# Attention by minimum of negated sums, in-order re-layouts, first products on half blocks behind a run on zeros, and a layer norm by square root without GpSimd, in a hybrid encoder layer

## Chip, cores and metric

One core of one Trainium2 chip. The metric is device time of one execution in microseconds (us), as a median over runs.

## What is computed

x is 2048 tokens by 1024 channels, float32. One input projection (1024 to 4608) feeds two mixers; their outputs, 1024 wide together, go through an output projection, and a layer norm closes:

```python
h = x @ w_in + b_in
q_a, k_a, v_a, g_a, q_h, z_fwd, z_bwd, i_h, g_h = split(h)
# group A, 8 heads of 64: neighbourhood attention on a 32 x 64 grid, window 8 x 16
s = q_a . k_a * 64 ** -0.5 + bias           # bias -inf outside the window
p = softmax(s);  o_a = (p . v_a) * silu(g_a)
# group B, 4 heads of 128: gated linear recurrence, one scan per direction
o_h = rms_norm(scan(q_h, k_f, i_h, f) + flip(scan(flip(...)))) * gain * silu(g_h)
y = concat(o_a, o_h) @ w_out + b_out
r = 2 ** 0.25 * x + y
out = (r - mean(r)) * rsqrt(var(r) + 1e-5) * ln_gain + ln_bias
```

## The kernel before

Products that need float32 accuracy are made of three: each operand is split into a high part, rounded to a shorter format (a cast on ScalarE, ACT), and the remainder (a subtraction on VectorE, DVE), and high x high, low x high and high x low are added up in PSUM. `split` (lines 154 and 155) does this for each piece that a DMA on SyncE's queue (SP) has brought.

Tokens come in four blocks of 512 (`TB`). A list of jobs, each 128 output channels for one block of tokens, makes up the input projection: 8 slices of the contraction (`KT`) times 3 products, 24 matmuls of 128 x 512. Jobs of values and gates (`vg`, `v2`) use 128 x 256 matmuls with tokens as rows. Around the jobs, eight units for each half of the tokens (4 recurrence heads, then 4 attention head pairs) do their own work. `projections()` is a generator: the units run, and between their steps `advance` takes so many matmuls of the jobs as filler. So the order on TensorE (PE) is written out by the program, and every matmul and transpose is tied to the one before by `in_order`. What the other engines do is ordered by a scheduler from data dependences and priorities, and each engine works its queue strictly in that order.

At the start, `first_loads` (lines 170 to 187) brings the weights of job 0 (`q` of the first recurrence head) in four pieces of 128 KB and the eight slices of the first token block, 256 KB each, in turns. Job 0 needs all of it. The x pieces land in the pool `raw`, which has 5 buffers, so the later ones wait until earlier ones have been split. Job 1 is `zf` (the forward gate) on the same tokens, with weights loaded by `load_w`; jobs 2 and 3 are `q` and `zf` on the second block.

When a job of attention's q or k is done, ACT copies it out of PSUM with the bias added and with its tokens re-ordered, so that 8 (or 4) rows of the grid at one column lie side by side (`evac_plain`, lines 220 and 222). It reads PSUM in order and writes SBUF with a stride:

```python
nc.scalar.activation(t.rearrange("p (c r) -> p r c", r=8), nat(ps), AF.Identity, bias=...)
```

In attention (`scores`, lines 711 to 726), for each step of 128 queries and two heads, DVE adds the bias to the scores in PSUM and takes the maximum per row (line 721), negates it (722), ACT takes the exponential with that as bias and the sum (723), and DVE divides (724, 725); PE transposes (`turn`), ACT copies (739), and PE multiplies with the values (`weigh`). The result is added to a bias and multiplied into the gate, in place, in the gate's own order (line 753): there the gate is read and written with a stride, and PSUM in order.

At the end comes the output projection, 4 token blocks of 4 tiles of 128 tokens, each with 24 matmuls per half of the channels, and the layer norm of `normalise`: statistics (`bn_stats`, `bn_aggr`), `rsqrt` by a shift and three Newton steps on DVE (lines 249 to 254, eleven small instructions), then subtract the mean and multiply by the gain (line 1003), and multiply by rstd and add the bias (1009), 512 columns at a time, and a store from SP's queue. For the last tile alone, ACT subtracts the mean (line 1000) and GpSimd (POOL) multiplies by the gain (line 1001).

Of the kernel before, what the change touches and what calls it, by code (L numbers as in the profile page):

```python
# [75 lines left out]
def _build():  # L76
# [18 lines left out]
    with tile.TileContext(nc) as tc, ExitStack() as top:  # L95
# [73 lines left out]

        def first_loads():  # L170

            w = wp.tile([P, 2, KT, P], F32R, tag="w", name="wt")
            wraw = [rawp.tile([P, KT // 2, P], F32, tag="raw", name="wraw") for _ in range(2)]
            tiles = []
            for kt in range(KT):
                if kt % 2 == 0:
                    i, o = kt // 4, kt % 4
                    part = wraw[i][:, o:o + 2]
                    nc.sync.dma_start(out=part, in_=w_in[16, :, kt:kt + 2])
                    nc.vector.tensor_copy(out=w[:, 0, kt:kt + 2], in_=part)  # L180
                    nc.vector.tensor_tensor(out=w[:, 1, kt:kt + 2], in0=part, in1=w[:, 0, kt:kt + 2].bitcast(F32), op=ALU.subtract)
                raw = rawp.tile([P, TB], F32, tag="raw", name="xraw")
                nc.sync.dma_start(out=raw, in_=xT_in[kt, :, 0:TB])
                t = xwp.tile([P, 2, TB], F32R, tag="xw", name="xt")
                split(t, raw)
                tiles.append(t)
            return w, tiles
# [101 lines left out]
        def projections():  # L289
# [20 lines left out]
            ws[0, "q"], xts[0] = first_loads()  # L310
            first_consts()
            for m, job in enumerate(jobs):
                n, what, c, tb, key = job
# [314 lines left out]
        def att_unit(half, u, h, ahead):  # L628
# [70 lines left out]
            def scores(j, g):  # L699
# [15 lines left out]
                for hd in range(2):  # L715
                    s = ss[hd]
                    sb = wk("ub", [P, 512])
                    mx = wk("mx", [P, 1], F32)
# [24 lines left out]
            def weigh(j, g):  # L743

                po = ps_tile("ms", "pov")
                for b in range(2):
# [239 lines left out]

        def normalise(rs):
# [5 lines left out]
            for i, (r, r0, stats) in enumerate(rs):  # L993
                nc.vector.bn_aggr(out=mv[:, i], in_=stats)
                if last:
                    nm = wk("nm", [P, 1])
                    nc.vector.tensor_scalar(out=nm, in0=mv[:, i, 0:1], scalar1=-1.0, scalar2=None, op0=ALU.mult)
                for cs in halves:
                    if last:
                        nc.scalar.activation(r[:, cs], r[:, cs], AF.Identity, bias=nm)  # L1000
                        nc.gpsimd.tensor_tensor(out=r[:, cs], in0=r[:, cs], in1=vec01[:, 1, cs], op=ALU.mult)
                    else:
                        nc.vector.scalar_tensor_tensor(out=r[:, cs], in0=r[:, cs], scalar=mv[:, i, 0:1], in1=vec01[:, 1, cs], op0=ALU.subtract, op1=ALU.mult)
            va = wk("va", [P, 2])
            nc.vector.tensor_scalar(out=va[:, 0:n], in0=mv[:, 0:n, 1], scalar1=LN_EPS, scalar2=None, op0=ALU.add)
            rstd = newton_rsqrt(va[:, 0:n], n, "ln")
            for i, (r, r0, stats) in enumerate(rs):
                for cs in halves:
                    nc.vector.scalar_tensor_tensor(out=r[:, cs], in0=r[:, cs], scalar=rstd[:, i:i + 1], in1=vec2[:, cs], op0=ALU.mult, op1=ALU.add)
                    nc.sync.dma_start(out=out[r0:r0 + P, cs], in_=r[:, cs])  # L1010
# [69 lines left out]
```

## Time and profile before

| what | value |
|---|---|
| time, median of 3 runs (range) | 1334.14 us (1333.4 to 1337.19) |
| the profiled execution's own time | 1335.69 us |
| span in the profile | 1333.9 us |
| PE busy | 1305.1 us, 98% |
| DVE busy | 894.6 us, 67% |
| ACT busy | 662.8 us, 50% |
| POOL busy | 67.4 us, 5% |
| chain that ended last | PE 89%, DVE 5%, ACT 2%, DMA 2%, issue 1% |

Busy time of PE includes the modelled length of pipelined matmuls, so 98% says that PE nearly always had work, not that it worked at its peak. The chain that ended last is followed back from the last instruction, at each step to what released it; what is not PE in it is where PE waited, and the ends of the program. The views used below are this chain, the timeline (instructions in order of time, with the idle time before them in brackets and what ended it), the list of PE's waits, the groups by line and shape, and stretches (busy time of each engine between two times).

### The profile page before, as it was taken

To read this page: it belongs to the slowest core of one execution; us is meant where nothing else is said; L and a number is where in the kernel's file an instruction comes from. 1 tells how busy PE (TensorE), PEld (TensorE's weight loads), DVE (VectorE), ACT (ScalarE), POOL (GpSimd) and SP (SyncE) were. 2 spreads that over 40 slices of the span, in tenths; PEclk is the share of its full clock that TensorE was granted. 3 is DMA by queue.
4 is the path that set the end of the run, shared out by engine and by line. 5 is a ranking of instruction groups with operands and counts; after the bars stand their busy time and mean duration, and the time that the engine had idled before them with its cause. 6 is when DMAs were issued, how large, how long until landed. Compare 5 with 4: busy or idle time off the path is not lost.

```text
span 1333.9 us, 25319 instructions
## 1 busy us (share of the span) xinstructions
PE 1305.1 (98%) x9864; PEld 1143.5 (86%) x9864; DVE 894.6 (67%) x2310; ACT 662.8 (50%) x1372; POOL 67.4 (5%) x126
## 2 busy tenths in 40 slices
PE   8999999999999999999999999999999999999996
PEld 6989898999888988989889898988889887788885
DVE  4385666575453364736868768688777778899757
ACT  4264444454464464534555646477776778631000
POOL 0000000011100100000000000000001000000000
PEclk9999999999999999999999999999999999999998
DMA  6121212123434365120323113365454667564201
GB/s 222 56 67 57 70 64 86 56 79 103 128 93 125 85 175 183 44 67 19 102 80 98 64 46 116 101 188 166 141 161 147 180 202 238 192 225 172 108 32 64
DMA packets 92312, 153.46 MB, mean 115 GB/s; under 512 B 9952, under 2 KB 42720, under 8 KB 92192
## 3 DMA queue, kind: packets, MB, share of 16 engines
q1 hardware_dynamic: 84256, 126.94, 30.1%
q0 software_dynamic: 7936, 24.91, 5.5%
q8 instruction: 77, 1.26, 0.4%
q14 instruction: 43, 0.35, 0.1%
HBM read 118.52 MB, written 33.29 MB: 114 GB/s over the span
## 4 chain that ended last, share of the span: by engine, by line
PE 89%; DVE 5%; ACT 2%; DMA 2%; issue 1%; SPq 0%; DVEq 0%; ACTq 0%
PE pj L139 36%; PE pv L139 20%; PE yp L139 13%; PE plev L139 4%; PE pov L139 4%; PE ptr L142 3%; PE S L139 3%; PE po L139 2%; PE pk L142 1%; PE pub L139 1%; PE pu L139 1%; PE pb L139 1%; DVE op L560 1%; DMA xraw<-in_xT_dram 1%; DVE ub L721 0%
## 5 line engine op out<-in xcount | busy, mean ns | idle before, releaser
L139 PE MATMUL pj<-xt,wt 128*128 128x512 f32 x2304 | 587.4, 400 | 7.3 <-ACT xt L154 5.7
L139 PEld LDWEIGHTS pj<-xt,wt 128*128 128x128 f32 x2304 | 419.1, 189 | 90.3 <-ACT xt L154 6.4
L139 PE MATMUL pv<-wv,xt 128*128 128x256 f32 x2304 | 301.4, 286 | 0.0
L139 PEld LDWEIGHTS pv<-wv,xt 128*128 128x128 f32 x2304 | 284.5, 191 | 3.0 <-issue 0.7
L139 PE MATMUL yp<-wo,chi 128*128 128x512 f32 (+1 forms) x528 | 161.3, 386 | 0.0
L471 ACT COPY km<-ST 128x512 f32<-128x512 f32 x96 | 64.3, 670 | 124.1 <-PE plev L139 78.9
L723 ACT ACTIVATE ub<-ub,nm 128x384 f32<-128x384 f32 (+2 forms) x128 | 78.8, 617 | 75.4 <-DVE nm L722 75.1
L139 PEld LDWEIGHTS yp<-wo,chi 128*128 128x128 f32 x528 | 98.1, 188 | 20.4 <-issue 0.7
L155 DVE TENSOR_TENSOR wt<-wraw,wt 128x512 fp32r<-128x512 f32 x82 | 53.9, 686 | 37.7 <-ACT wt L154 37.3
L482 DVE TENSOR_TENSOR ST<-ST,PX 128x512 f32<-128x512 f32 x96 | 66.0, 688 | 16.2 <-ACT qm L473 15.6
L739 ACT COPY op<-ptr 96x384 f32<-96x384 f32 (+3 forms) x128 | 62.0, 526 | 14.0 <-PE ptr L142 13.7
L483 DVE TENSOR_TENSOR ST<-ST,PX 128x512 f32<-128x512 f32 x96 | 65.6, 683 | 0.0
L473 ACT COPY qm<-ST 128x512 f32<-128x512 f32 x96 | 64.0, 667 | 0.0
L142 PE MATMUL ptr<-ident,ub 128*128 128x128 f32 (+1 forms) x448 | 59.6, 273 | 2.9 <-DVE ub L725 2.1
L155 DVE TENSOR_TENSOR wv<-vraw,wv 128x512 fp32r<-128x512 f32 x48 | 31.3, 688 | 46.1 <-ACT wv L154 45.9
L142 PEld LDWEIGHTS ptr<-ident,ub 128*128 128x128 f32 (+1 forms) x448 | 51.3, 133 | 11.1 <-DVE ub L725 2.9
L457 DVE COPY_PREDICATED AH<-masks,plev 128x256 f32<-128x256 uint8 x96 | 42.8, 446 | 26.6 <-PE plev L139 24.3
L230 ACT ACTIVATE ht<-pj,bs_sb 128x512 f32<-128x512 f32 x48 | 33.0, 687 | 52.1 <-PE pj L139 52.0
L154 ACT CAST wt<-wraw 128x512 fp32r<-128x512 f32 x82 | 47.7, 621 | 15.3 <-PE pv L139 8.6
L725 DVE TENSOR_SCALAR ub<-ub,rs 128x384 f32<-128x384 f32 (+2 forms) x128 | 52.5, 423 | 2.9
L139 PE MATMUL plev<-qm,km 128*64 128x64 f32 x1536 | 51.0, 223 | 0.0
L139 PEld LDWEIGHTS plev<-qm,km 128*64 128x64 f32 x1536 | 47.5, 138 | 3.7 <-issue 2.5
(212 smaller groups left out, 1791.0 us busy)
## 6 DMA issues: line engine op xcount, KB each, us to landing
wraw<-in_w_in_dram SPq DMA_DIRECT2D x100, 256.0 KB, 2.8
vraw<-in_w_v_dram SPq DMA_DIRECT2D x48, 256.0 KB, 2.8
xraw<-in_xT_dram SPq DMA_DIRECT2D x32, 256.0 KB, 3.9
craw<-cat SPq DMA_DIRECT2D x32, 256.0 KB, 3.7
PP<-in_rpb_dram SPq DMA_DIRECT2D x16, 384.0 KB, 3.7
PX<-in_rpb_dram SPq DMA_DIRECT2D x16, 384.0 KB, 3.5
vt<-hv POOLq DMA_DIRECT2D x32, 128.0 KB, 2.6
PP<-in_rpb_dram SPq DMA_DIRECT2D x8, 512.0 KB, 3.5
```

What stands on the lines that cost most here:

```text
L139: in_order(nc.tensor.matmul(out, lhsT=lhsT, rhs=rhs, start=start, stop=stop, **kw))
L142: in_order(nc.tensor.transpose(out=out, in_=in_, identity=ident))
L154: nc.scalar.copy(out=hi, in_=raw)
L155: last_split[0] = nc.vector.tensor_tensor(out=lo, in0=raw, in1=hi.bitcast(F32), op=ALU.subtract)
L457: nc.vector.copy_predicated(AH, masks[:, l].unsqueeze(1).to_broadcast([P, 4, HC]), pl)
L471: nc.scalar.copy(out=km.rearrange("p (n h b) -> p n h b", h=2, b=B), in_=mix(ST, 0, 3, B, 0, TB))
L473: nc.scalar.copy(out=qm.rearrange("p (n h b) -> p n h b", h=2, b=B), in_=mix(ST, 1, 2, B, 0, TB))
L482: nc.vector.tensor_tensor(out=S1, in0=S1, in1=pr[:, :, :, 0].unsqueeze(3).to_broadcast([P, 2, m, B]), op=ALU.mult)
L483: nc.vector.tensor_tensor(out=S2, in0=S2, in1=pr[:, :, :, 1].unsqueeze(3).to_broadcast([P, 2, m, B]), op=ALU.mult)
L723: nc.scalar.activation(sb[:, 0:nk], sb[:, 0:nk], AF.Exp, bias=nm, accum_out=sums[:, hd:hd + 1])
L725: nc.vector.tensor_scalar(out=sb[:, 0:nk], in0=sb[:, 0:nk], scalar1=rs[:, hd:hd + 1], scalar2=None, op0=ALU.mult)
L739: nc.scalar.copy(out=PT[0:n, 0:nch].rearrange("p a b -> p (a b)"), in_=pt[0:n, 0:nch * P])
```

## The change

It does five things.

- **Start.** `warm` sets a tile to zero on DVE and multiplies it with itself on PE, seven times 128 x 256 in plain float32, before any load has landed. The result is not used.
- **First products on half blocks.** `first_loads` brings the first token block in two halves of 256 tokens: weights of `q` and the first half in turns (the first two slices alone, the others two in one DMA), then the weights of `zf`, then the second half. The x pieces land in the pool `h` (17 buffers) instead of `raw`. The weights' high parts are now cast by ACT, not DVE. Jobs 0 and 1 become 96 matmuls of 128 x 256 in the order `q` first half, `zf` first half, `q` second half, `zf` second half. The second token block is asked for right behind (`prepare(jobs[2])`).
- **Re-layouts in order.** The evacuations of q and k, and the product with the gate, now write SBUF in order (q and k) or in runs of 32 (gate), and read PSUM with a stride.
- **Minimum of negated sums.** Line 721 makes the negated sum and takes the minimum, which is the negated maximum; the exponential has scale -1. The negation (722) goes.
- **Layer norm.** The eleven small instructions become a square root on ACT, a reciprocal and one Newton step (three instructions) on DVE. In the last tile DVE does what ACT and POOL did, in the order: centre the first half, centre and store the second half last, in two pieces of 256 columns, the first of them stored from ACT's queue.

```diff
+        def warm():
+
+            z = wk("AH", [P, 4, HC], F32).rearrange("p a b -> p (a b)")
+            nc.vector.memset(z, 0.0)
+            ps = ps_tile("ms", "warm")
+            for _ in range(7):
+                mm(ps[:, 0:256], z[:, 0:P], z, True, True)
...
         def first_loads():
...
+            def half(o, kt, n):
+                cs = slice(o * 256, o * 256 + 256)
+                raw = h_tile("xraw").rearrange("p (k t) -> p k t", k=2)
+                nc.sync.dma_start(out=raw[:, 0:n], in_=xT_in[kt:kt + n, :, cs].rearrange("k p t -> p k t"))
+                for k in range(n):
+                    split(tiles[kt + k][:, :, cs], raw[:, k])
+
+            for kt in range(0, KT, 2):
+                part = wraw[kt // 4][:, kt % 4:kt % 4 + 2]
+                nc.sync.dma_start(out=part, in_=w_in[16, :, kt:kt + 2])
+                split(wa[:, :, kt:kt + 2], part)
+                if kt == 0:
+                    half(0, 0, 1)
+                    half(0, 1, 1)
+                else:
+                    half(0, kt, 2)
+            wb = load_w(20)
+            for kt in range(0, KT, 2):
+                half(1, kt, 2)
+            return wa, wb, tiles
...
-                nc.scalar.activation(t.rearrange("p (c r) -> p r c", r=8), nat(ps), AF.Identity, bias=b_sb[:, c:c + 1])
+                nc.scalar.activation(t.rearrange("p (c r) -> p c r", r=8), ps.rearrange("p (r c) -> p c r", c=COLS), AF.Identity, bias=b_sb[:, c:c + 1])
...
-                    t.rearrange("p (a c r) -> p a r c", a=2, r=4),
-                    ps.rearrange("p (a r c) -> p a r c", a=2, r=4),
+                    t.rearrange("p (a c r) -> p a c r", a=2, r=4),
+                    ps.rearrange("p (a r c) -> p a c r", a=2, r=4),
...
+            warm()
+            ws[0, "q"], ws[0, "zf"], xts[0] = first_loads()
             first_consts()
+            prepare(jobs[2])
...
-                        nc.vector.tensor_tensor_reduce(out=sb[:, 0:nk], in0=s[:, 0:nk], in1=bt[:, hd, 0:nk], scale=1.0, scalar=-3e38, op0=ALU.add, op1=ALU.max, accum_out=mx)
-                        nc.vector.tensor_scalar(out=nm, in0=mx, scalar1=-1.0, scalar2=None, op0=ALU.mult)
-                        nc.scalar.activation(sb[:, 0:nk], sb[:, 0:nk], AF.Exp, bias=nm, accum_out=sums[:, hd:hd + 1])
+                        nc.vector.tensor_tensor_reduce(out=sb[:, 0:nk], in0=s[:, 0:nk], in1=bt[:, hd, 0:nk], scale=-1.0, scalar=3e38, op0=ALU.add, op1=ALU.min, accum_out=nm)
+                        nc.scalar.activation(sb[:, 0:nk], sb[:, 0:nk], AF.Exp, bias=nm, scale=-1.0, accum_out=sums[:, hd:hd + 1])
...
-                gate = nat(h["g", g])[:, :, 16 * j:16 * j + 32].rearrange("p r c -> p c r")
+                gate = nat(h["g", g])[:, :, 16 * j:16 * j + 32]
...
-                    out=gate, in0=po[:, 0:2 * P].rearrange("p (c r) -> p c r", r=8), scalar=b_sb[:, 8 + u:9 + u],
+                    out=gate, in0=po[:, 0:2 * P].rearrange("p (c r) -> p r c", r=8), scalar=b_sb[:, 8 + u:9 + u],
...
+            root = wk("va", [P, 2])[:, 0:n]
+            nc.scalar.activation(root, mv[:, 0:n, 1], AF.Sqrt, bias=eps)
...
+            early = [(i, cs) for i in range(n) for cs in halves]
+            late = []
+            if last:
+                early, late = early[:-1], [early[-1]]
+            for i, cs in early:
+                centre(i, cs)
...
+            nc.vector.reciprocal(out=rstd, in_=root)
+            nc.vector.tensor_tensor(out=a, in0=rstd, in1=rstd, op=ALU.mult)
+            nc.vector.scalar_tensor_tensor(out=a, in0=a, scalar=-0.5, in1=va, op0=ALU.mult, op1=ALU.mult)
+            nc.vector.scalar_tensor_tensor(out=rstd, in0=a, scalar=1.5, in1=rstd, op0=ALU.add, op1=ALU.mult)
+            for i, cs in early:
+                store(i, cs, nc.sync)
+            for i, cs in late:
+                centre(i, cs)
+                for k, queue in enumerate((nc.scalar, nc.sync)):
+                    store(i, slice(cs.start + 256 * k, cs.start + 256 * k + 256), queue)
```

Three places show how the order moves. On PE, the start of the program, as a difference (`pj` and `pv` are the banks of jobs, `xt` and `wt` split x and weights, `AH` the zeros):

```order
 L95 UNCONDITIONAL_BRANCH
-L139 MATMUL pj<-xt,wt 128x512 x144
+L139 MATMUL warm<-AH 128x256 x7
+L139 MATMUL pj<-xt,wt 128x256 x96
+L139 MATMUL pj<-xt,wt 128x512 x96
 L139 MATMUL pv<-wv,xt 128x256 x192
```

Seven products on zeros stand in front, and 48 of the first 144 matmuls are cut in two; but for bank numbers nothing else of PE's order differs.

On DVE, a step of attention in the first half, before (`S` scores, `PX` the bias, `ub` the result, `mx` and `nm` the maximum and its negation, `rs` the reciprocal of the sum):

```order
L721 ISA ub,mx<-S,PX 128x384
L721 ISA mx 128x1
L721 ISA ub,mx<-S,PX 128x384
L721 ISA mx 128x1
L722 TENSOR_SCALAR nm<-mx 128x1 x2
L724 RECIPROCAL rs<-sums 128x1
L725 TENSOR_SCALAR ub<-ub,rs 128x384
```

and the same step in the change:

```order
L754 ISA ub,nm<-S,PX 128x384
L754 ISA nm 128x1
L754 ISA ub,nm<-S,PX 128x384
L754 ISA nm 128x1
L756 RECIPROCAL rs<-sums 128x1
L757 TENSOR_SCALAR ub<-ub,rs 128x384
```

The two negations are gone; the rest stands as it stood, though elsewhere splits and other DVE work move by a few places around such steps.

On DVE, the last tile's layer norm in the change, from the aggregated statistics (`mv`) to the end:

```order
L1029 BN_AGGR mv<-stats 128x2
L1034 TENSOR_SCALAR nmr<-mv 128x1
L1038 SCALAR_TENSOR_TENSOR xpair<-xpair,mv,ST 128x512
L1053 RECIPROCAL lny<-va 128x1
L1038 SCALAR_TENSOR_TENSOR xpair<-xpair,mv,ST 128x512
L1054 TENSOR_TENSOR lna<-lny 128x1
L1055 SCALAR_TENSOR_TENSOR lna<-lna,nmr 128x1
L1056 SCALAR_TENSOR_TENSOR lny<-lna,lny 128x1
L1042 SCALAR_TENSOR_TENSOR xpair<-xpair,lny,PP 128x512
L1042 SCALAR_TENSOR_TENSOR xpair<-xpair,lny,PP 128x256 x2
```

Ten instructions after the statistics' own, where before stood thirteen small ones and two of 512 columns, with ACT and POOL beside them; the scheduler has put the second half's centring between the reciprocal and the Newton step.

## Rows read from the trace of the kernel before

**Rows 1.** Page, busy time: engine, us, share of the span, instructions.
```profile
PE 1305.1 (98%) x9864; PEld 1143.5 (86%) x9864; DVE 894.6 (67%) x2310; ACT 662.8 (50%) x1372; POOL 67.4 (5%) x126
```

**Rows 2.** Chain that ended last, first 66 us: start us, us, what.
```profile
7.88 3.88 DMA xraw<-in_xT_dram
12.46 30.64 PE pj L139 x132
43.10 23.03 PE pv L139 x192
```

**Rows 3.** Timeline, first 60 us: start us, us, engine, line, operation, tiles [idle before].
```profile
0.73 1.28 ACT L154 ACT_TABLE_LOAD   x1 [0.73 <-PEq L77]
...
3.20 0.43 DVE L181 TENSOR_TENSOR wt<-wraw,wt 128x256 fp32r<-128x256 f32 x1
...
5.50 1.22 PE L139 MATMUL pj<-xt,wt 128*128 128x512 f32 x2 [5.50 <-ACT xt L154]
...
26.82 0.69 ACT L218 ACTIVATE hp<-pj,b_sb 128x512 f32<-128x512 f32 x1 [1.63 <-PE pj L139]
...
32.26 0.69 ACT L230 ACTIVATE ht<-pj,bs_sb 128x512 f32<-128x512 f32 x1 [3.72 <-PE pj L139]
```

**Rows 4.** Timeline, PE alone, 9 to 12 us.
```profile
8.63 3.62 PE L139 MATMUL pj<-xt,wt 128*128 128x512 f32 x8
```

**Rows 5.** Stretch 4 to 6 us: engines' busy us (x), PEclk, DMA share, GB/s.
```profile
4.00:6.00 2.00, 0.50 (x1) 0.50 (x2) 0.00 (x0) 0.79 (x2) 0.00 (x0) 1.00 0.96 335
```

**Rows 6.** PE's waits, whole span: who <- for whom: us in total, times, longest us.
```profile
PE pk L142 <- DVE ST L483: 2.5, 2, 2.2
PE ptr L142 <- DVE ub L725: 2.1, 2, 1.7
PE S L139 <- ACT hu L236: 1.9, 1, 1.9
PE S L139 <- DVE ST L682: 1.9, 2, 1.1
```

**Rows 7.** Groups by line and shape: xcount, busy us, mean ns, idle before.
```profile
L681 ACT CAST ST<-hp 64x256 fp32r<-64x256 f32 x56 | 20.6, 402 | 6.6 <-PE S L139 6.1
L155 DVE TENSOR_TENSOR xt<-xraw,xt 128x512 fp32r<-128x512 f32 x32 | 21.5, 690 | 12.2 <-ACT xt L154 11.9
L220 ACT ACTIVATE hp<-pj,b_sb 128x512 f32<-128x512 f32 x16 | 19.9, 1244 | 17.9 <-PE pj L139 17.7
L222 ACT ACTIVATE hp<-pj,b_sb 128x512 f32<-128x512 f32 x16 | 19.1, 1193 | 14.4 <-PE pj L139 14.4
L722 DVE TENSOR_SCALAR nm<-mx 128x1 f32<-128x1 f32 x128 | 17.4, 149 | 0.3
L753 DVE SCALAR_TENSOR_TENSOR hu<-pov,b_sb,hu 128x256 f32<-128x256 f32 x24 | 16.2, 676 | 21.0 <-PE pov L139 20.8
L363 DVE TENSOR_TENSOR hv<-pv,bvg 128x256 f32<-128x256 f32 x32 | 13.4, 419 | 40.2 <-PE pv L139 40.2
L218 ACT ACTIVATE hp<-pj,b_sb 128x512 f32<-128x512 f32 x16 | 11.0, 688 | 27.4 <-PE pj L139 27.4
```

**Rows 8.** Stretch 835.2 to 838.5 us, columns as in rows 5.
```profile
835.20:838.50 3.30, 3.23 (x12) 2.97 (x13) 3.22 (x8) 2.48 (x6) 0.00 (x0) 0.50 0.36 99
```

**Rows 9.** Chain that ended last, from 1322 us on.
```profile
1322.74 0.43 DVE xpair L1038
...
1323.66 0.28 DVE mv L994
...
1327.87 0.17 DVE lna L252
```

**Rows 10.** Timeline from 1324 us on, PE left out.
```profile
1324.14 1.33 ACT L1000 ACTIVATE xpair<-xpair,nm 128x512 f32<-128x512 f32 x2 [87.69 <-DVE nm L997]
...
1324.95 2.48 POOL L1001 TENSOR_TENSOR xpair<-xpair,ST 128x512 f32<-128x512 f32 x2 [155.80 <-DVE lna L253]
...
1328.53 1.41 DVE L1009 SCALAR_TENSOR_TENSOR xpair<-xpair,lny,PP 128x512 f32<-128x512 f32 x2
```

More of the change, by code (lines that the diff above doesn't have):

```diff
@@ L168, in load_x @@
             return tiles
+        def warm():
[4 more added lines that the diff above has]
+                mm(ps[:, 0:256], z[:, 0:P], z, True, True)
         def first_loads():
-            w = wp.tile([P, 2, KT, P], F32R, tag="w", name="wt")
+            wa = wp.tile([P, 2, KT, P], F32R, tag="w", name="wt")
             wraw = [rawp.tile([P, KT // 2, P], F32, tag="raw", name="wraw") for _ in range(2)]
[L174 to L187, printed above, removed]
+            tiles = [xwp.tile([P, 2, TB], F32R, tag="xw", name="xt") for _ in range(KT)]
+            def half(o, kt, n):
[17 more added lines that the diff above has]
+            return wa, wb, tiles
         def load_w(c):
@@ L308, in prepare @@
                     ws[key] = load_w(c)
-            ws[0, "q"], xts[0] = first_loads()
+            warm()
+            ws[0, "q"], ws[0, "zf"], xts[0] = first_loads()
             first_consts()
+            prepare(jobs[2])
+            banks = [ps_tile("pj", "pj"), ps_tile("pj", "pj")]
+            for o in range(2):
+                cs = slice(o * 256, o * 256 + 256)
+                for ps, what in zip(banks, ("q", "zf")):
+                    w = ws[0, what]
+                    for kt in range(KT):
+                        for i, (a, b) in enumerate(((0, 0), (1, 0), (0, 1))):
+                            mm(ps[:, cs], w[:, a, kt], xts[0][kt][:, b, cs], kt == 0 and i == 0, kt == KT - 1 and i == 2)
+                            if (kt * 3 + i) % 2 and not (o == 1 and kt == KT - 1 and i == 2):
+                                yield 1
+                    if o == 1:
+                        gots[0][what, 0] = evac_plain(ps, 16) if what == "q" else evac_tanh(ps, 20)
+                        yield 1
             for m, job in enumerate(jobs):
+                if m < 2:
+                    continue
                 n, what, c, tb, key = job
@@ L717, in scores @@
                     sb = wk("ub", [P, 512])
-                    mx = wk("mx", [P, 1], F32)
                     nm = wk("nm", [P, 1], F32)
                     with tc.high_priority(offset=PRIO):
-                        nc.vector.tensor_tensor_reduce(out=sb[:, 0:nk], in0=s[:, 0:nk], in1=bt[:, hd, 0:nk], scale=1.0, scalar=-3e38, op0=ALU.add, op1=ALU.max, accum_out=mx)
-                        nc.vector.tensor_scalar(out=nm, in0=mx, scalar1=-1.0, scalar2=None, op0=ALU.mult)
-                        nc.scalar.activation(sb[:, 0:nk], sb[:, 0:nk], AF.Exp, bias=nm, accum_out=sums[:, hd:hd + 1])
+                        nc.vector.tensor_tensor_reduce(out=sb[:, 0:nk], in0=s[:, 0:nk], in1=bt[:, hd, 0:nk], scale=-1.0, scalar=3e38, op0=ALU.add, op1=ALU.min, accum_out=nm)
+                        nc.scalar.activation(sb[:, 0:nk], sb[:, 0:nk], AF.Exp, bias=nm, scale=-1.0, accum_out=sums[:, hd:hd + 1])
                         nc.vector.reciprocal(out=rs[:, hd:hd + 1], in_=sums[:, hd:hd + 1])
@@ L985, in _build @@
         nc.sync.dma_start(out=vec2, in_=vec_in[2])
+        eps = cp.tile([P, 1], F32, name="eps")
+        nc.vector.memset(eps, LN_EPS)
         def normalise(rs):
@@ L994, in normalise @@
                 nc.vector.bn_aggr(out=mv[:, i], in_=stats)
[L995 to L1010, printed above, removed]
+            root = wk("va", [P, 2])[:, 0:n]
@@ new lines, in normalise, with centre, store @@
+            nc.scalar.activation(root, mv[:, 0:n, 1], AF.Sqrt, bias=eps)
+            va = wk("nmr", [P, 2])[:, 0:n]
+            nc.vector.tensor_scalar(out=va, in0=mv[:, 0:n, 1], scalar1=LN_EPS, scalar2=None, op0=ALU.add)
+            def centre(i, cs):
+                r = rs[i][0]
+                nc.vector.scalar_tensor_tensor(out=r[:, cs], in0=r[:, cs], scalar=mv[:, i, 0:1], in1=vec01[:, 1, cs], op0=ALU.subtract, op1=ALU.mult)
+            def store(i, cs, queue):
+                r, r0, _ = rs[i]
+                nc.vector.scalar_tensor_tensor(out=r[:, cs], in0=r[:, cs], scalar=rstd[:, i:i + 1], in1=vec2[:, cs], op0=ALU.mult, op1=ALU.add)
+                queue.dma_start(out=out[r0:r0 + P, cs], in_=r[:, cs])
@@ new lines, in normalise @@
+            early = [(i, cs) for i in range(n) for cs in halves]
[4 more added lines that the diff above has]
+                centre(i, cs)
+            rstd = wk("lny", [P, 2])[:, 0:n]
+            a = wk("lna", [P, 2])[:, 0:n]
+            nc.vector.reciprocal(out=rstd, in_=root)
+            nc.vector.tensor_tensor(out=a, in0=rstd, in1=rstd, op=ALU.mult)
+            nc.vector.scalar_tensor_tensor(out=a, in0=a, scalar=-0.5, in1=va, op0=ALU.mult, op1=ALU.mult)
```

## Prediction
> **What bounds the kernel now.** I read the page first: PE has work for 98% of the span [rows 1], so an edit pays only where PE waits or where the program has not begun or has ended on PE. Next the chain that ended last: from 12.46 us it is PE with hardly a break [rows 2], and ahead of that it is DMA, the last wait being for a slice of x that took 3.88 us to land. Third the list of PE's waits: after the start, its four largest entries come to 8.4 us in 7 waits, over a run of 1,300 us [rows 6]. Fourth the end: the first DVE step after PE's last matmul is at 1322.74, and from there it is DVE, with ACT and POOL beside it, until 1329.94 [rows 9, 10]; then the last store lands. So there are three places: a head of some 12 us, some 10 us of waits inside, and a tail of 11 us. PE's order in between is the same before and after.
>
> **The head.** How much PE lost there is read from the first full-speed jobs. The third job's result is taken out at 26.82, the next at 32.26 [rows 3]: 5.44 us for 24 matmuls, 227 ns each. So the third job began at 26.82 - 5.44 = 21.38, with two jobs (10.9 us of work at that pace) behind it: 10.5 us were lost. Part is the wait for data (first product at 5.50, [rows 3]); part is pace: between 8.63 and 12.25 eight matmuls took 3.62 us [rows 4], which with the last one's own length taken off is 0.43 us each, 512 columns at 1.2 GHz, the lower of the clock's two levels, though the column for the granted clock already prints 1.00 [rows 5].
>
> After the change, the first half of `q` needs 1.5 MB instead of 2.5. DMA brings 335 GB/s where it is not held up [rows 5], so it is in about 4.5 us after the first piece (about 2.9), at 7.4 (2.9 being 3.20 of [rows 3] less a cast). But each of the 12 pieces must pass ACT and DVE. DVE's subtraction of 256 columns takes 0.43 [rows 3], ACT's cast at most about 0.40 (nearest row, 64 x 256, [rows 7]); with 0.02 of issue, 12 x 0.45 = 5.4 us from 3.3 on, the first cast being done then: 8.7. DVE is the limit, and PE's 24 matmuls of 256 columns (120 ns at full clock by the `pv` row, 23.03 us for 192 [rows 2]; 0.21 at the lower level) fit beside it. `q`'s first half ends at 8.9. Then DVE makes the low parts of `zf`'s weights, 2 x 0.69 [rows 7], the first at 9.4: `zf`'s first half runs from about 9.4 to 12.3 (24 x 0.12). The second half of x, 8 x 0.45 on DVE, is ready at 13.7, ahead of need (its last slice at 14.8). The other 48 matmuls end at 12.3 + 5.8 = 18.0. The third job starts at 18.0 instead of 21.38: **-3.4 us**. That includes the price of cutting in two, 96 x 0.12 against 48 x 0.227, +0.6. The second token block is next: 5 MB in all at 335 GB/s are in at about 18.4, and its last slice is needed 7/8 into that job, at 22.8; in the ACT queue the evacuation of `zf` stands ahead of two of its casts, to about 18.6, which leaves time. Ends: if DVE were no limit, 7.4 in place of 8.7, -4.6; if the clock stays at the lower level until 12.5, when it rose before, `zf`'s first half takes about 1.4 us longer, -2.0. I take -3.4, since the zeros and the first half together keep PE at work from about 1 us on, where before it began at 5.5.
>
> The zeros cost nothing: by my estimate seven products of two passes each at 0.21 fill about 1 to 4 us, the first real product could start at 3.7 at the earliest, and no one else waits for them. The weights' four casts go from DVE to ACT and are counted above.
>
> **Inside.** DVE loses 128 negations of 149 ns [rows 7]; ACT's 32 evacuations may fall from 1244 and 1193 ns to the plain form's 688, 17 us in all, and the 32 gate products from 676 to the 419 of the plain 256-column form, 8 us [rows 7]. Nearly all of this lies beside PE's fillers and is worth nothing. What counts is the list of waits [rows 6]. Three entries, 5.9 us in 5 waits, are attention's (transposes for `ub`, scores for `ST` and `hu`); in each, DVE's or ACT's queue is behind, and one step's two negations, 0.3 us, or an evacuation's 0.5 in front of it go. The `pk` wait (2.2) has an evacuation on ACT in its chain as well. 5 x 0.3 + 0.5 = **-2.0 us**. Bounds: nothing, or worse, since the scheduler also moves splits and other DVE work by some places (+1, about one such wait of [rows 6] more), and -6 if most of these waits go together with the stretch at 835.2, where PE, after waiting, ran 3.3 us at 0.50 of its clock [rows 8] (1.65 us at most).
>
> No row shows PSUM read with a stride, so the re-layouts are bounded from both sides: 688 ns (the stride was the whole cost) and 1244 (it costs as much on the reading side). Even the latter adds nothing to the sum; it takes the 0.5 out, so the sum would be 0.5 higher. I take a value near 688, as the operation, its 512 elements and its engine are the plain form's [rows 7]. The Trainium skill, "SBUF — State Buffer", section "Door 1: The DMA port swizzle", speaks against: it gives PSUM lines of 8 bytes, against 16 in SBUF, and says that access that is not contiguous slows matmuls a good deal. By this rule of the Trainium skill the strided read would be no better than the strided write, and no gain is left on ACT; no row here shows it. What that would lead to is a rival below.
>
> **The tail.** Before, from the end of the statistics (1323.66 + 0.28 = 1323.94) to the end of DVE's last product (1328.53 + 1.41 = 1329.94) it is 6.0 us [rows 9, 10], of it 1.41 the two products at the end and the rest small instructions and their waits, with POOL multiplying for 2.48 beside them. After: one small instruction (0.17), centre 0.75, reciprocal 0.17, centre 0.75, three small ones at 0.19, store product 0.75, two of 256 columns at 0.45: 4.05. The square root lies on ACT beside the first centring. That is -1.95. The last transfer is 128 KB instead of 256, 0.4 us at 335 GB/s [rows 5]: **-2.35 us**. The square root needs one table load more on ACT; before its first use, with the first pair of tiles of the output projection, and none after it. At 1.28 us [rows 3] that is hidden: ACT's last work ahead of the tail was over 87.69 us before it [rows 10], two token blocks ahead, and the casts that it delays are needed a whole block later. If that cover were gone it would cost 1.28.
>
> **Sum.** -3.4 - 2.0 - 2.35 = -7.8 us. Against the profiled execution's own 1335.69 that is 1327.9; that one stood 1.55 above the median of the three runs. I put the base in the middle, 1334.9, and forecast **1327 us**, own range 1324 to 1330.
>
> **Rivals.**
> - *The clock rises no earlier.* For it: between 5.5 and 12 us PE did work, and stayed at 0.43 us a matmul [rows 4]. Against: it worked with gaps then. Head -2.0 in place of -3.4: 1328.5. Chance 0.13.
> - *Nothing inside.* The waits stay or one is added, because order on DVE and ACT is the scheduler's. For it: 7 waits are few, and each may move. 1334.9 - 3.4 - 2.35 + 1 = 1330. Chance 0.20.
> - *Most waits go.* 1334.9 - 3.4 - 2.35 - 6 = 1323. Chance 0.08.
> - *Slower: PSUM read with a stride stalls ACT.* ACT works its queue in order, so a long evacuation holds back the exponentials and copies that PE waits for. To come out 4 us slower it must eat 7.8 + 3.2 = 11 us. If all 32 evacuations reached PE, 0.35 us more each would do; the waits of [rows 6] say that hardly one in four does, so it decides from about 1244 + 1400 = 2.6 us an evacuation, and the time is then 1338 or more. No row comes near 2.6. The rule of the Trainium skill cited above ("SBUF — State Buffer") points this way, without a size. Chance 0.07.
>
> **How the numbers follow.** Forecast 0.52, rivals 0.13, 0.20, 0.08, 0.07. About 0.3%, 4 us, is what a measurement of this kernel can tell from no change, so faster means below 1330.1: nearly all of the forecast (0.49), most of the first rival (0.10), a third of the second (0.07), all of the third: 0.74. Slower is the last: 0.07; the rest, 0.19, is no change. The range of 8 in 10 takes in forecast, both middle rivals and most of the third: 1322 to 1332.
>
> **What would show it.** Third job's result out of PSUM at about 23.4 instead of 26.8; matmuls of 256 columns 0.12 apart from 9 us on; evacuations near 0.69 us and gate products near 0.42; the waits of [rows 6] 2 us less in sum; 4 us from statistics to DVE's last product, and the span's end 2.3 us sooner after PE's. I am wrong if the 256-column products still run 0.21 apart at 10 us, if evacuations are longer than before, or if PE's waits inside grow by several us.

## The result, and the profile after

| | before | after |
|---|---|---|
| time, median (range, runs) | 1335.24 us (1333.4 to 1337.19, 4) | 1324.82 us (1324.38 to 1324.98, 4) |
| the profiled execution's own time | 1335.69 us | 1324.98 us |
| third job's result taken out of PSUM | 26.82 | 26.09 |
| first DVE step after PE's last matmul | 1322.74 | 1315.23 |

The ratio is 0.9921 with a 95% interval of [0.9904, 0.9938]: faster by 0.8%. The forecast was 1327, the range 1322 to 1332. The two profiled executions split the gain at the same two places where the prediction split it:

| part | how it is read | measured | forecast |
|---|---|---|---|
| head | 26.09 - 26.82 | -0.7 | -3.4 |
| inside | (1315.23 - 26.09) - (1322.74 - 26.82) | -6.8 | -2.0 |
| tail | (1324.98 - 1315.23) - (1335.69 - 1322.74) | -3.2 | -2.35 |
| sum | | -10.7 | -7.8 |

So the total is near and the parts are not: the head gave a fifth of what was forecast, the inside over three times as much, and the two misses (2.7 us one way, 4.8 the other) nearly cancel.

**The head.** The timeline of the change, PE and ACT only:

```profile
1.19 6.12 PE L139 MATMUL warm<-AH 128*128 128x256 f32 x14 [1.19 <-DVE eps L1020]
...
6.97 2.50 PE L139 MATMUL pj<-xt,wt 128*128 128x256 f32 x18
...
10.14 1.32 PE L139 MATMUL pj<-xt,wt 128*128 128x256 f32 x7 [0.68 <-ACT xt L154]
...
11.72 21.62 PE L139 MATMUL pj<-xt,wt 128*128 128x256 f32 x127 [0.26 <-DVE wt L155]
...
26.09 0.69 ACT L235 ACTIVATE hp<-pj,b_sb 128x512 f32<-128x512 f32 x1 [1.31 <-PE pj L139]
...
31.56 0.69 ACT L247 ACTIVATE ht<-pj,bs_sb 128x512 f32<-128x512 f32 x1 [3.75 <-PE pj L139]
```

These answer to [rows 3]. The zeros take 14 passes, 0.43 us each, and hold PE to 7 us, not to 4. Six of the seven products from 10.14 on end the first half of `q`; the seventh is the first of `zf`, whose others run from 11.72 on, where the forecast had about 9.4. That is 2.3 us. 31.56 - 26.09 = 5.47 is again one job, so the third job began at 20.6, against 18.0 forecast and 21.38 before: 2.6 late, the last 0.3 of it being 71 products in 8.9 us instead of 8.6. The chain of the first 45 us says why `zf` came late:

```profile
3.58 0.43 SPq L188
...
4.06 0.47 SPq L194
...
4.57 5.09 DMA xraw<-in_xT_dram
...
9.68 0.71 ACT xt L154 x2
...
11.72 30.69 PE pj L139 x167
```

`SPq` is SP's queue issuing loads. Each issue takes 0.4 to 0.5 us, one after the other from 0.74 on, so the last piece of the first half is asked for only at about 4.5, and then needs 5.09 us to land, while the loads asked for behind it are under way too. Behind the landing come the casts on ACT, of x and then of `zf`'s weights, and a subtraction on DVE, 2.0 us together. In the stretch 7 to 8.5 us DMA's share is 0.97, and PE is at its full clock by its pace (14 products of 256 columns, 0.107 us each; before, PE was at the lower level until after 12 us, [rows 4]):

```profile
7.00:8.50 1.50, 1.50 (x14) 1.48 (x13) 1.39 (x4) 1.35 (x6) 0.00 (x0) 1.00 0.97 281
```

**Inside.** PE's waits over the whole span, to be held against [rows 6]:

```profile
PE pk L142 <- DVE ST L517: 1.9, 1, 1.9
...
PE ptr L142 <- DVE nm L754: 0.5, 1, 0.5
PE S L139 <- ACT ub L755: 0.5, 1, 0.5
```

Of before's four entries `pk` stands, and the three of attention are gone or small. Attention's waits of [rows 6] all lie in the stretch 890 to 1140 us; its row before the change, in the columns of [rows 5]:

```profile
890.00:1140.00 250.00, 243.31 (x1771) 207.21 (x1770) 198.04 (x620) 188.86 (x428) 12.26 (x22) 1.00 0.57 175
```

and of the change, with the row that answers to [rows 8]:

```profile
835.20:838.50 3.30, 3.30 (x24) 3.02 (x23) 3.21 (x10) 2.30 (x5) 0.00 (x0) 1.00 0.51 159
890.00:1140.00 250.00, 248.57 (x1820) 211.83 (x1820) 189.90 (x538) 186.39 (x434) 12.60 (x22) 1.00 0.60 181
```

PE without work went from 250 - 243.31 = 6.7 us to 1.4, which is 5.3 of the 6.8 us. The rest is the stretch at 835.2: before it ran at 0.50 of the clock, here at 1.00, up to 1.65 us. What the longest wait for `ub` was behind, before the change, the timeline shows:

```profile
1129.88 0.62 ACT L898 CAST chi<-craw 128x512 fp32r<-128x512 f32 x1 [1.46 <-DMA craw<-cat]
...
1130.53 0.69 DVE L905 TENSOR_TENSOR clo<-craw,chi 128x512 fp32r<-128x512 f32 x1 [1.39 <-ACT chi L898]
...
1131.13 0.87 DVE L725 TENSOR_SCALAR ub<-ub,rs 128x512 f32<-128x512 f32 x2
...
1131.67 1.11 PE L142 MATMUL ptr<-ident,ub 128*128 128x128 f32 x8 [1.67 <-DVE ub L725]
```

The division that PE waits for stands in DVE's queue behind a subtraction for the output projection, that one behind a cast on ACT, and the cast waits 1.46 us for a load. The two negations of this step are not what is last here; the place in the queue is.

**The re-layouts and the gate**, groups by line and shape:

```profile
L237 ACT ACTIVATE hp<-pj,b_sb 128x512 f32<-128x512 f32 x16 | 11.0, 690 | 19.7 <-PE pj L139 19.6
L235 ACT ACTIVATE hp<-pj,b_sb 128x512 f32<-128x512 f32 x16 | 11.0, 688 | 29.2 <-PE pj L139 29.2
L239 ACT ACTIVATE hp<-pj,b_sb 128x512 f32<-128x512 f32 x16 | 11.0, 685 | 14.7 <-PE pj L139 14.7
...
L785 DVE SCALAR_TENSOR_TENSOR hu<-pov,b_sb,hu 128x256 f32<-128x256 f32 x24 | 11.6, 482 | 25.5 <-PE pov L139 25.2
```

Lines 237 and 239 were 1244 and 1193 ns [rows 7]; they now cost what the plain line 235 costs. The gate product went from 676 to 482 ns, not to 419.

**The tail**, the timeline from PE's last result on:

```profile
1315.23 0.42 DVE L1090 TENSOR_TENSOR xpair<-xpair,yp 128x256 f32<-128x256 f32 x1 [1.98 <-PE yp L139]
...
1316.15 0.26 DVE L1029 BATCH_NORM_AGGREGATE mv<-stats 128x2 f32<-128x24 f32 x1
...
1316.51 0.29 ACT L1032 ACTIVATE va<-mv,eps 128x1 f32<-128x1 f32 x1 [10.44 <-DVE mv L1029]
1316.52 0.74 DVE L1038 SCALAR_TENSOR_TENSOR xpair<-xpair,mv,ST 128x512 f32<-128x512 f32 x1
...
1317.25 0.73 DVE L1038 SCALAR_TENSOR_TENSOR xpair<-xpair,mv,ST 128x512 f32<-128x512 f32 x1
...
1318.28 0.16 DVE L1056 SCALAR_TENSOR_TENSOR lny<-lna,lny 128x1 f32<-128x1 f32 x1
1318.48 1.54 DVE L1042 SCALAR_TENSOR_TENSOR xpair<-xpair,lny,PP 128x512 f32<-128x512 f32 x3
```

From the end of the statistics (1316.41) to the end of DVE's last product (1320.02) it is 3.6 us, against 6.0 before; the square root (0.29) lies beside the first centring. From there to the end of the execution it is 4.96, against 5.75 [rows 10].

### The profile page after: what moved, and what is told of

Read it like the earlier page. It is cut to its first block, busy times and chain, and to the rows that moved or that the text cites. A ratio compares the mean times of both kernels' runs of the same rounds, so it can differ in the third digit from the quotient of the medians.

```text
span 1323.2 us, 25289 instructions
## 1 busy us (share of the span) xinstructions
PE 1307.6 (99%) x9926; PEld 1148.4 (87%) x9926; DVE 865.0 (65%) x2127; ACT 652.8 (49%) x1392; POOL 65.2 (5%) x124
## 3 DMA queue, kind: packets, MB, share of 16 engines
q8 instruction: 78, 1.28, 0.4%
## 4 chain that ended last, share of the span: by engine, by line
PE 88%; DVE 5%; ACT 4%; DMA 1%; issue 1%; SPq 0%; DVEq 0%; ACTq 0%
PE pj L139 35%; PE pv L139 20%; PE yp L139 13%; PE plev L139 4%; PE pov L139 4%; PE ptr L142 3%; PE S L139 3%; PE po L139 2%; PE pk L142 1%; PE pub L139 1%; PE pu L139 1%; PE pb L139 1%; ACT ub L755 1%; DVE op L594 1%; DVE ub L754 1%
## 5 line engine op out<-in xcount | busy, mean ns | idle before, releaser
L139 PE MATMUL pj<-xt,wt 128*128 128x512 f32 (+1 forms) x2352 | 584.6, 394 | 1.7 <-ACT hv L402 0.7
L155 DVE TENSOR_TENSOR wt<-wraw,wt 128x512 fp32r<-128x512 f32 (+1 forms) x86 | 55.4, 673 | 43.7 <-ACT wt L154 42.9
L154 ACT CAST wt<-wraw 128x512 fp32r<-128x512 f32 (+1 forms) x86 | 48.8, 609 | 14.8 <-PE pv L139 9.7
L1032 ACT ACTIVATE va<-mv,eps 128x2 f32<-128x2 f32 (+1 forms) x9 | 2.7, 296 | 106.2 <-DVE mv L1029 106.2
```

The lines of the kernel that those rows point to most:

```text
L139: in_order(nc.tensor.matmul(out, lhsT=lhsT, rhs=rhs, start=start, stop=stop, **kw))
L154: nc.scalar.copy(out=hi, in_=raw)
L155: last_split[0] = nc.vector.tensor_tensor(out=lo, in0=raw, in1=hi.bitcast(F32), op=ALU.subtract)
```

## The experiments

Twelve kernels, timed against the kernel before on the same chip (its median there 1335.7 to 1336.3). The change itself was timed beside a median of 1335.24, so a difference between its median and another's is good to about 1 us. "Idle" is 250 us less PE's busy time in the stretch 890 to 1140 of the profiled execution, one for each kernel.

| kernel | median (range) | ratio, interval | idle |
|---|---|---|---|
| before | | | 6.7 |
| the change | 1324.82 (1324.38 to 1324.98) | 0.9921 [0.9904, 0.9938] | 1.4 |
| new start alone | 1334.6 (1331.32 to 1335.96) | 0.9985 [0.9976, 0.9994] | 5.2 |
| minimum alone | 1330.46 (1329.32 to 1331.31) | 0.9956 [0.9939, 0.9973] | 2.9 |
| re-layouts alone | 1334.91 (1332.1 to 1336.09) | 0.9992 [0.9983, 1.0002] | 6.0 |
| gate alone | 1335.16 (1333.42 to 1337.89) | 0.9995 [0.9986, 1.0005] | 5.9 |
| layer norm alone | 1332.43 (1330.21 to 1334.11) | 0.9973 [0.9964, 0.9983] | 6.7 |
| change without new start | 1327.79 (1326.58 to 1328.48) | 0.9939 [0.9922, 0.9955] | 1.9 |
| change without zeros | 1326.42 (1324.65 to 1326.83) | 0.9927 [0.9912, 0.9942] | 1.7 |
| change with three zeros | 1325.19 (1324.01 to 1327.13) | 0.9922 [0.9907, 0.9937] | 1.4 |
| change, maximum and negation back | 1328.95 (1328.86 to 1330.74) | 0.9952 [0.9938, 0.9965] | 4.5 |
| change, three zeros, weights from two queues | 1324.71 (1323.65 to 1325.07) | 0.9914 [0.9901, 0.9928] | 1.5 |
| change, unused negation | 1328.48 (1327.15 to 1329.9) | 0.9938 [0.9921, 0.9955] | 5.1 |
| change, negation on POOL | 1329.51 (1328.95 to 1331.13) | 0.9951 [0.9936, 0.9966] | 4.3 |

### The start

*The new start alone*, on the kernel before: `warm`, `first_loads` and the 96 half products as in the change's diff.

```diff
-            ws[0, "q"], xts[0] = first_loads()
+            warm()
+            ws[0, "q"], ws[0, "zf"], xts[0] = first_loads()
```

> The kernel before with the new start alone (zeros, half blocks, new order of loads). Theory 'inside': the start is worth only the 0.7 us that the third job's result came sooner (26.09 against 26.82), and the 6.8 us gained between there and PE's last matmul come from the other parts; then PE's last matmul ends at about 1322.0 and the time is 0.7 us below before. Rival 'shift': what was gained inside (the stretch at half clock at 835 us gone, the waits near 1130 us gone) came from the start's shift of everything by 0.7 us, since whether the clock falls depends on when PE pauses; then this kernel too lacks the half-clock stretch and is 2 to 6 us faster than before.

The third job's result came at 25.96, 0.9 us sooner than before, and the median is 1.1 us lower (the ratio says 2.0, between 0.8 and 3.2). The profiled execution is the fastest of ten: it kept the full clock at 835, and its idle is 1.5 us less. Whether the new start had a part in these two was not shown. Ten runs spread over 4.6 us, so the median is what counts.

The head is better read from all traces: in the six executions with the old start the third job's result came between 26.61 and 28.32 (median 26.91), in the five with the new start and seven zeros between 25.96 and 28.12 (median 26.17). So the gain of 0.7 us stands, and a single head can be 2 us off.

*The change without the new start*: the same lines the other way round.

> The change with the start of the kernel before. Theory 'inside': all but 0.7 us of the 10.4 us gain stays, third job's result at 26.8, PE's waits inside as in the change, time about 1325.5. Rival 'shift': the half-clock stretch near 835 us comes back and with it 1.5 us, the waits near 1130 us with up to 4 us; 1327 to 1331.

3.0 us slower than the change. The traces account for it: the third job's result at 26.91 (+0.8), idle 1.9 in place of 1.4 (+0.5), and the half clock is back:

```profile
831.00:835.00 4.00, 2.13 (x30) 1.52 (x27) 3.92 (x8) 1.83 (x4) 0.00 (x0) 1.00 0.32 129
835.20:838.50 3.30, 3.30 (x13) 2.91 (x12) 3.19 (x8) 2.84 (x6) 0.00 (x0) 0.50 0.45 150
```

PE was busy for 2.13 of the 4 us ahead of it; so it was in the change, at the same place, and there no fall followed. So what the new start gives is 0.7 to 0.9 us at the head; most of the rest of the 3 us, in these two executions, hangs on whether the clock falls far behind it.

*The change without zeros.*

```diff
-            warm()
```

> The change without the products on zeros. Theory 'data': the first half's last piece of x lands at about 9.7 us whatever PE did before, the first real product starts at about 4.3, and the third job's result comes at 26.1 plus or minus 0.3. Theory 'clock': PE's clock rose to its upper level at 6.96 us because PE had been at work from 1.2 us; without zeros it rises only after about 11 us, the 256-column products run 0.21 apart until then, and the third job's result comes 1 to 2.5 us later, 27 to 28.5.

The loss that the theory of the clock expected came. Its timeline:

```profile
4.07 1.68 PE L139 MATMUL pj<-xt,wt 128*128 128x256 f32 x6 [4.07 <-ACT xt L154]
...
6.94 2.96 PE L139 MATMUL pj<-xt,wt 128*128 128x256 f32 x12 [1.19 <-ACT xt L154]
...
28.02 0.69 ACT L235 ACTIVATE hp<-pj,b_sb 128x512 f32<-128x512 f32 x1 [2.61 <-PE pj L139]
```

The first real product starts at 4.07, 2.9 us sooner than in the change, and still the third job's result is 1.9 us later. The last piece of x landed 0.3 us later than in the change. The rest is PE's clock, as its pace shows: 9 products in the 2 us from 7 to 9, 17 in the 1.8 us from 16.2 to 18.

```profile
7.00:9.00 2.00, 2.00 (x9) 2.00 (x10) 2.00 (x6) 1.49 (x5) 0.00 (x0) 1.00 0.91 262
16.20:18.00 1.80, 1.80 (x17) 1.80 (x16) 0.82 (x2) 0.09 (x1) 0.00 (x0) 1.00 0.53 181
```

28.02 is later than most heads with the old start too, so in this trace the half blocks alone, without an early clock, brought nothing. No version has zeros in front of the old blocks.

*Three zeros in place of seven.*

```diff
-            for _ in range(7):
+            for _ in range(3):
```

> The change with three products on zeros instead of seven: they end at about 3.8 us, just ahead of the first real product. Theory 'data': no change in the third job's result (26.1). Theory 'clock': PE is at work from 1.2 us nearly without a gap, so the clock rises at about the same 7 us and the result comes at 26.1 too, or, where the real products come with too many gaps behind the zeros, as late as without zeros.

The third job's result came at 25.78, 0.3 us sooner than with seven, and the last piece of x landed 0.5 us sooner in that execution; the medians, 1325.19 and 1324.82, are equal within their ranges. PE's real products begin earlier but wait for the same pieces of x. Seven are not too many, and three are not too few.

*Weights from two queues*: three zeros, and two of the weight pieces issued from ACT's queue, so that SP asks for x earlier.

```diff
-                nc.sync.dma_start(out=part, in_=w_in[16, :, kt:kt + 2])
+                (nc.scalar if kt in (2, 4) else nc.sync).dma_start(out=part, in_=w_in[16, :, kt:kt + 2])
```

> The change with three products on zeros, and two of the four pieces of the first weights issued from ACT's queue, so that the last piece of x that the first half needs is issued at about 3.6 us instead of 4.57. If its landing (9.66 in the change, 5.1 us after its issue) is set by the issue, it lands at 8.7 and the third job's result comes at about 25 instead of 26.1; time about 1 us below the change. If it is set by what the DMA engines move in all (2 MB are in by then), it lands at 9.5 or later and nothing moves.

The mechanism held: the last piece was in by 8.7. In the chain SP's row of issues is no longer in front of PE:

```profile
1.19 3.47 DMA xraw<-in_xT_dram
...
5.14 36.14 PE pj L139 x192
```

and the third job's result came at 25.00, 1.1 us sooner than in the change and 0.8 sooner than with three zeros alone, which is the like comparison. The profiled time gained nothing, for in this execution the clock fell again after the pause at 831:

```profile
832.90:836.20 3.30, 3.30 (x12) 2.82 (x11) 3.15 (x8) 2.81 (x6) 0.00 (x0) 0.50 0.56 156
```

The medians are equal (1324.71 and 1324.82), so this version is no faster by measurement; its fastest run, 1323.65, is 0.7 below the change's fastest.

### Attention

*The minimum alone*, on the kernel before: lines 721 to 723 as in the change's diff.

> The kernel before with the minimum of negated sums alone. PE's waits between 890 and 1140 us are 6.7 us before and 1.9 us in the change. Theory 'negation': the 128 negations stood in DVE's queue ahead of the splits and products that PE waits for, so this alone takes those waits to about 2 us and the time 4 to 5 us down. Rival 'evacuation': the waits end on ACT's queue or behind it, and leave only with the shorter evacuations; then this takes 1 us or less.

5.4 us of the median, half of the whole gain, and idle from 6.7 to 2.9. DVE's instructions in the stretch went from 620 to 538. Its profiled execution kept the full clock at 835, which is up to 1.65 us beside the 3.8 of idle.

*The re-layouts alone* (lines 220 and 222), and *the gate alone* (line 753), each on the kernel before, as in the change's diff.

> The kernel before with the in-order evacuations of q and k alone (1244 and 1193 ns to about 690). Theory 'negation': PE's waits between 890 and 1140 us stay above 5 us, time within 1 us of before. Rival 'evacuation': they fall to about 3 us and the time by 3 to 4 us.

> The kernel before with the gate product re-ordered alone (676 to about 480 ns, 32 times). Both theories: DVE is 6 us less busy, PE's waits move by less than 1 us and the time by less than 1 us.

Both are within the measurement of no change, though the evacuations take 17 us less on ACT and the gate products 6 less on DVE. Idle hardly moves: 6.0 and 5.9.

*Maximum and negation back in the change.*

```diff
-  ... scale=-1.0, scalar=3e38, op0=ALU.add, op1=ALU.min, accum_out=nm)
+  ... scale=1.0, scalar=-3e38, op0=ALU.add, op1=ALU.max, accum_out=mx)
+                        nc.vector.tensor_scalar(out=nm, in0=mx, scalar1=-1.0, scalar2=None, op0=ALU.mult)
```

> The change with the maximum and its negation put back, all else as in the change. If the negations are what PE waited behind, PE's waits between 890 and 1140 us go from 1.9 us to 5 us or more and the time is 4 to 6 us above the change, about 1330. If the other parts had made the negation harmless (shorter evacuations, another order), it is less than 2 us above.

The median is 4.1 us above the change. The profiled execution is 3.9 above, and not all of it is attention's: its third job's result is at 28.12, 2.0 us late, because the last piece of the first half landed later and the clock fell once more at 12 us. Behind the head it is 1.9 us, with idle at 4.5 against 1.4; that 3.1 us of idle cost only 1.9 is explained in part (the change has a wait of 0.7 us for `rQg`, outside the stretch, that this version has not). Waits for `ST` and `hu`, as before the change, are back:

```profile
PE S L139 <- ACT hu L253: 1.9, 1, 1.9
...
PE S L139 <- DVE ST L716: 1.1, 1, 1.1
```

*Is it DVE's queue or the exponential's start?* Two kernels keep one half each of what a negation does. The first leaves the minimum and adds a negation that nobody reads, on DVE; the second has the maximum back and negates on POOL.

```diff
+                        nc.vector.tensor_scalar(out=mx, in0=nm, scalar1=-1.0, scalar2=None, op0=ALU.mult)
```

> The changed kernel with one more instruction on DVE after each minimum: its negation, into a tile that nobody reads (computes the same). DVE's queue is as long as before the change, but the exponential waits for the minimum alone. Theory 'queue': what the negations cost was their 128 places in DVE's in-order queue, ahead of subtractions and masks that PE waits for: the waits between 890 and 1140 come back, from 1.4 us of PE without work to about 4.5 (what the version with maximum and negation shows), and the time is 1327 to 1329. Theory 'chain': the cost was that the exponential started one instruction later: PE is without work for at most 2 us there, and the time is 1324.5 to 1325.5.

```diff
-                        nc.vector.tensor_scalar(out=nm, in0=mx, scalar1=-1.0, scalar2=None, op0=ALU.mult)
+                        nc.gpsimd.tensor_scalar(out=nm, in0=mx, scalar1=-1.0, scalar2=None, op0=ALU.mult)
```

> The changed kernel with the maximum back and its negation done by POOL instead of DVE (computes the same). DVE's queue is as short as in the change, but the exponential waits for one more instruction and two hand-overs between engines. Theory 'queue': PE is without work for about 1.4 to 2 us between 890 and 1140, and the time is 1324.5 to 1326. Theory 'chain': the path from the maximum to the exponential is longer than it was before the change, so PE is without work for 4.5 us or more there, and the time is 1328 or more. Both may hold in part; then this one and the unused negation share the 4 us between them.

Both kernels lose more than half of the gain in attention: with the unused negation the time is 1328.48 and idle 5.1, with the negation on POOL 1329.51 and 4.3, though DVE has 535 instructions in the stretch there, as few as in the change. By these times each half would be enough. But about half of the idle in each is one wait, 2.5 and 2.6 us, that neither theory speaks of. The rows of the stretch, for the first

```profile
890.00:1140.00 250.00, 244.94 (x1799) 208.61 (x1798) 194.33 (x625) 184.70 (x433) 12.20 (x22) 1.00 0.58 177
```

and the second, with the group of the negations on POOL, 298 ns each against 149 on DVE [rows 7], and a stretch just behind its longest wait:

```profile
890.00:1140.00 250.00, 245.68 (x1798) 209.67 (x1797) 188.78 (x535) 185.46 (x431) 40.96 (x112) 0.99 0.58 177
...
L756 POOL TENSOR_SCALAR nm<-mx 128x1 f32<-128x1 f32 x128 | 37.5, 298 | 212.8 <-DVE mx L755 190.7 <-ACT chi L932 7.4 <-ACT wo L154 5.0
...
PE ptr L142 <- ACT op L773: 2.6, 1, 2.6
...
1120.40:1123.60 3.20, 3.20 (x9) 2.53 (x8) 3.15 (x7) 3.15 (x8) 1.32 (x2) 0.50 0.51 130
```

That last row is a second place where a wait of over 2 us was followed by the half clock. The wait itself, with the unused negation and then with POOL's:

```profile
1115.62 0.62 ACT L154 CAST wo<-woraw 128x512 fp32r<-128x512 f32 x1 [1.04 <-DMA woraw<-in_w_out_dram]
...
1116.92 0.61 ACT L757 ACTIVATE ub<-ub,nm 128x384 f32<-128x384 f32 x1
...
1119.66 0.64 PE L142 MATMUL ptr<-ident,ub 128*96 128x128 f32 x4 [2.54 <-ACT op L773]
```

```profile
1117.20 0.62 ACT L932 CAST chi<-craw 128x512 fp32r<-128x512 f32 x1 [1.52 <-DMA craw<-cat]
...
1117.72 0.61 ACT L757 ACTIVATE ub<-ub,nm 128x384 f32<-128x384 f32 x1
...
1118.95 0.64 PE L142 MATMUL ptr<-ident,ub 128*96 128x128 f32 x4 [2.57 <-ACT op L773]
```

In both the second head's exponential could have begun over 3 us sooner: its operand was there at 1113.5 (the minimum) and at 1113.1 (POOL's negation). It stands in ACT's queue behind casts that wait for a load. In the change the two exponentials of this step follow each other at 1112.63 and 1113.25, and PE does not wait. So this wait comes from a new order on ACT, as the one of 1.67 us before the change came from the order on DVE, and neither a full DVE queue nor a later exponential is shown to be enough by itself.

What is shown is that the instruction matters, one way or the other: all versions with an instruction more in a step lose 4.3 us or more in the stretch, all with the change's attention 1.9 or less, the minimum alone 2.9. The wait for `hu` is 1.9 us in five of the six executions with maximum and negation on DVE (0.7 with the re-layouts alone), and in no other is it among the stretch's longest waits. What stays open: every version is also a new order by the scheduler, and idle is made of four or five waits, so how much of it is the negation itself and how much the order that came with it was not separated.

### The layer norm alone

On the kernel before, `normalise` as in the change's diff.

> The kernel before with the new layer norm alone. From DVE's first step after PE's last matmul to its last product 4.8 us instead of 7.2, and the end of the span 0.8 us sooner behind that, as the last store is half as large: time 3.2 us below before, PE's last matmul where it was. Rival: DVE's work inside the output projection had held PE up as well, and PE's last matmul ends sooner too; or the casts that now stand behind square roots in ACT's queue make PE wait, and part of the 3.2 us goes.

3.4 us of the median; the change's trace has -3.2 for its tail. Idle is as before (6.7), so nothing of this part's gain is inside.

The five parts alone come to -1.1 - 5.4 - 0.9 - 0.7 - 3.4 = -11.5 us, the change to -10.4 in its medians (by the ratios, -13 and -10.6): the parts add up to within what these measurements tell, two of the five being no change by themselves.

## Why the prediction was right, and where its steps were wrong

- **The three places and the sum.** Right in kind: head, inside and tail are where the time went, and the rest of the 1,300 us stayed. The total was held by a head sized too large and an inside sized too small; that these two nearly cancelled is luck. Inside, what happened is the rival "Most waits go", which had a chance of 0.08.
- **The head, -3.4.** The step that failed is "it is in about 4.5 us after the first piece (about 2.9), at 7.4", with "DVE is the limit" behind it. Taking DMA's rate as the limit left out that one queue issues the loads one by one, 0.4 to 0.5 us each, and that a load then took 5.09 us to land: the last piece of the first half landed at 9.66. The version with two queues, 0.8 us sooner than its like with three zeros, shows the issue's share; what the loads asked for behind it took of the 5.09 us was not separated. DVE was no limit: it was idle for 0.82 us ahead of that piece. Two small slips in the working do not bear on this: 1.5 times 1,048,576 bytes at 335 GB/s take 4.7 us, not 4.5, and without DVE's limit the head would be -4.7, not -4.6.
- **The zeros.** "Two passes each at 0.21" was half the size; a pass took 0.43 at the lower level. "The zeros cost nothing" holds all the same, since three do as well as seven. That they are what lets the clock rise early was right, and the rival with the late clock is what the version without them shows: 1.9 us at the head in one trace, 1.6 in the median of four runs.
- **Inside, -2.0.** The mechanism was right (waits of attention go, 17 us of evacuation beside PE's fillers are worth nothing), the size was not. The term that failed is "one step's two negations, 0.3 us" per wait. It took each wait to shrink by what its own step had lost, and the waits went whole: idle fell by 5.3 us, 3.8 of it with the minimum alone. With the stretch at 835.2, which kept its clock in this profile, the inside came to -6.8, beyond the bound of -6. The traces show why a wait is not made of its own step: the longest for `ub`, 1.67 us, stood behind a cast that waited for a load. Why the shorter step moved these waits as a whole stays open.
- **Evacuations.** Expected near 0.69, measured 690 and 685 ns. The Trainium skill's rule on PSUM's 8-byte lines ("SBUF — State Buffer", section "Door 1: The DMA port swizzle") speaks of matmuls. Carried over to ACT's reads, as the prediction did, it would have left no gain; for these reads the measurement decides against it. Only the gate product, at 482 against the 419 of another form, may hold a small price for stride. So the slower rival's price, 2.6 us an evacuation and more, is far from what was measured.
- **The tail, -2.35.** Right in its order, 0.85 short: 3.6 us instead of 4.05 from the statistics to DVE's last product, since reciprocal and small instructions overlap the centrings, and the end behind it 0.8 us shorter instead of 0.4. The table load was hidden as forecast (1.28 us at 1170 us, ahead of the first square root).

## What to carry to other kernels

Where PE waits seldom, do not cost an edit in attention by its own length at the few waits alone: two instructions of 149 ns in each step, with the order that came with them, were worth about 3 to 5 us here, 17 us of evacuation nothing that could be measured. Follow each long wait back through the queues first: here two kinds of it ended at a cast that waited for a load, with an exponential or a division in line behind it. At a program's start, count the issues in one DMA queue as well as the bytes. And before a gain of 1 to 2 us is put down to an edit, look at the granted clock behind PE's longest pauses in both profiles.

## What the runs showed of the hardware that was not expected

- A pass of a plain float32 product of 256 columns on zeros took 0.43 us at the lower clock level, twice the 0.21 of the other products of that length there; the profile counts two passes for each (14 in 6.12 us in the change).
- After a pause of PE of about 2 us the granted clock sometimes fell to 0.50 and sometimes not. At the same pause near 832 us it fell in the profiled executions of before, of layer norm alone, of the change without its start and with two queues, with the unused negation and with POOL's; it did not in those of the change and of seven others. Behind waits between 1116 and 1137 us it fell with the re-layouts alone, the layer norm alone and the negation on POOL. What decides it was not tried.
- ACT reading PSUM with a stride and writing SBUF in order: 690 and 685 ns. Reading in order and writing with a stride: 1244 and 1193 [rows 7].
